# A top-k zone whose weight splits move to GpSimd and whose VectorE queue is written in program order

## The chip, the cores and the metric

The kernel runs on one core of a Trainium2 chip. The metric is the time of one execution on the device, in microseconds (us); the time before is the median of three runs. In the profile PE is TensorE (its weight loads are shown apart, as PEld), DVE is VectorE, ACT is ScalarE, POOL is GpSimd and SP is SyncE, which issues most of the loads.

## The reference

Two layers, each a mixer (a gated linear recurrence and sparse attention) and then an expert retrieval (PEER). Only the second part is cut out here; the change's main work is in its first half. One load of the mixer, the gate weights `lru_wa` and `lru_wx`, is touched too.

```
q = (xf @ wq).reshape(T, 8, 2, 128)                  # T = 256 tokens, 8 heads
s = einsum('thcd,ckd->thck', q, subkeys)             # 128 keys in each half c
sv, si = top_k(s, 16)
cand = sv[:, :, 0, :, None] + sv[:, :, 1, None, :]   # 16 x 16 sums
cv, ci = top_k(cand, 16)
experts = si[0][ci // 16] * 128 + si[1][ci % 16]
gate = softmax(cv)
act = gelu(einsum('cd,ced->ce', xc, u_tab[experts]))
y = einsum('ce,ced->cd', act * gate, v_tab[experts])
```

The layer ends with a residual sum and a layer norm, and the second layer does the same with weights of its own.

## The kernel before

**Dense instead of gathered.** The kernel computes the products with all 16384 rows of `u_tab` (128 tiles of 128 rows, `u_tile(0)` to `u_tile(127)`), keeps their gelu, and later multiplies them with gates that are zero for experts not chosen. So the u tiles depend on no list, and the matmuls of PE can run while DVE makes the lists.

**A weight tile** (`wtile`, L95) is 128x1024 f32. SP loads it into `raw` (four buffers), ACT casts it to `hi` (L104), and another engine subtracts, `lo = raw - hi` (L105); `hi` and `lo` have three buffers each. A narrow tile (`col_mm`, L113) is eight chunks of three matmuls of 256 columns, the third of which reads `lo`; a wide one (`col_mm2`, L122 and L123) is eight chunks of one matmul of 512 columns and one of 256, and DVE adds its two halves (L757). Tiles below `NWIDE` are narrow. The split of a u tile below `NPOOL` and of the weights of queries 2 and 3 is POOL's, every other one DVE's.

**The top-k zone** is what lies inside the pool `topk`. `query(h)` makes the projection of a head, `top(h)` its scores (eight matmuls, L815), a copy of them by ACT into `ss` (L817) and four lists of 16 on DVE, each five operations in `best16` (L801): MAX8, FIND_INDEX8, MATCH_REPLACE8, MAX8, FIND_INDEX8. The profile shows a MATCH_VALUE_LOAD ahead of each of the latter two kinds. For a group of four heads `pairs(g)` adds candidates (nine sums, L829 and L833, into `cd`) and makes eight lists of 50 columns; `choices(g)` does the index work on 2048-element tiles. `turn_round` transposes the results on PE and casts them.

**What sets the order.** `work()` is a generator that issues the zone's work in pieces and yields a cost after each; the loop behind it issues u tiles until these costs are covered:

```
                a, room = 0, 0.0
                for cost in work():
                    room -= cost
                    while room < 0 and a < 96:
                        u_tile(a)
                        room += 2.88 if a < NPOOL else 1.66
```

A scheduler of the language then settles the order on each engine; on DVE operations that do not depend on each other pass one another. Behind the zone comes the dense part, where the gate matrices are built and the other u tiles run.

**The mixer** is issued by a list of tokens per layer, `ORDER[l]`; `d1` calls `const_load(1)`, which loads `lw`, the gate weights of the recurrence (512 KB, L677), and `d2`, `d3` load others. In layer 1 the matmuls at L377 are the first to read `lw`.

Of the kernel before, what the change touches and what calls it, by code (L numbers as in the profile page):

```python
# [16 lines left out]
AF = mybir.ActivationFunctionType  # L17
# [3 lines left out]
D = 1024  # L21
# [28 lines left out]
NPOOL = 14  # L50
NWIDE = 40
# [27 lines left out]
def trunk_kernel(ctx: ExitStack, tc: tile.TileContext, x, xt, cst, lam, pvec, brow, w_in, w_lx, w_v, w_q4, lru_w,  # L79
# [193 lines left out]
    for l in range(NL):  # L273
# [461 lines left out]
        with tc.tile_pool(name="peer", bufs=1, reuse_waits="tile") as pp:  # L735
# [10 lines left out]
            def u_tile(a):  # L746
                if a % 2 == 0:
                    ub[a] = bank() if a < NWIDE else act_tile()
                w = wtile(u_tab[l, a], (8, 128), POOL if a < NPOOL else DVE)
                if a < NWIDE:  # L750
                    ps = ub[a - a % 2]
                    col_mm(ps[:, HALF[a % 2]], w, xT)
                else:
                    ps, at = bank(), ub[a - a % 2]
                    col_mm2(ps, w, xT)
                    ACT.copy(at[:, a % 2], ps[:, S:])  # L756
                    DVE.tensor_tensor(at[:, a % 2], at[:, a % 2], ps[:, :S], op=ALU.add)  # L757
                if a % 2:
                    if a < NWIDE:
                        at = act_tile()  # L760
                        ACT.activation(at.rearrange("p a b -> p (a b)"), ps, AF.Gelu_apprx_tanh)
                    else:
                        ACT.activation(at, at, AF.Gelu_apprx_tanh)  # L763
                    kept[a - 1] = spill.tile([128, 2, S], F32, name="kept%d" % (a - 1), bufs=1)
                    ACT.dma_start(kept[a - 1], at)

            with tc.tile_pool(name="topk", bufs=1, reuse_waits="tile") as tk:
# [17 lines left out]
                def query(h):  # L785
# [4 lines left out]
                    else:  # L790
                        ps = bank()
                        for c in range(2):
                            k = 2 * h + c - 4
                            if "w%d" % k in W:
                                raw_mm(ps[:, c * 256:c * 256 + 256], W["w%d" % k])
                            else:
                                col_mm(ps[:, c * 256:c * 256 + 256], wtile(wq[l, k], (8, 128), POOL if h < 4 else DVE), xT)
# [10 lines left out]
                def top(h):  # L808

                    qh = qhs.pop(h)  # L810
# [6 lines left out]
                    ACT.copy(ss.rearrange("p a b -> p (a b)"), ps)  # L817
                    s2 = tk.tile([128, 4, 128], F32, name="s2", bufs=2)
                    for tb in range(2):
# [75 lines left out]
                def turn_round():  # L895
                    for w in range(3):
# [4 lines left out]
                        tok = ps[:, :256].rearrange("p (q i) -> p q i", i=2)  # L901
# [7 lines left out]
                def work():  # L909
                    for h in (2, 0, 1, 3):  # L910
                        yield from top(h)
                    yield from pairs(0)
                    query(4)
                    yield 2.44 - 5.76
                    for h in range(4, 8):
                        if h < 7:
                            query(h + 1)
                            yield 2.44 - 5.76
                        yield from top(h)
                    yield from pairs(1)  # L920
                    yield from choices(0)
                    yield from choices(1)
                    yield 1.0
# [7 lines left out]
                a, room = 0, 0.0  # L931
                for cost in work():
                    room -= cost
                    while room < 0 and a < 96:
                        u_tile(a)
                        room += 2.88 if a < NPOOL else 1.66
                        a += 1

            with tc.tile_pool(name="dense", bufs=1, reuse_waits="tile") as dp:
# [37 lines left out]

                a0 = a
                made = onehots(0)
                for i in range(32):  # L980
                    following = onehots(8 * i + 8) if i < 31 else None
                    while a < 128 - NLATE and (a - a0) * 32 < (i + 1) * (128 - NLATE - a0):
                        u_tile(a)
# [100 lines left out]
                for a in range(128 - NLATE, 128):  # L1084
                    u_tile(a)
# [211 lines left out]
```

## Time and profile before

| | before |
|---|---|
| runs | 1926.81, 1930.38, 1931.85 us; median 1930.38 |
| profiled execution | 1928.28 us, of which its span is 1926.5 |
| granted TensorE clock, mean over the span | 0.992 |
| busy share of the span | PE 98%, DVE 72%, ACT 53%, POOL 4% |
| longest sums of PE's waits | 20.8 us for `lo` of DVE before L113 (nine waits, longest 4.0), 4.6 for a load before L239, 3.9 before L377 |
| top-k zones | from PE's first narrow u or query tile to its first wide tile: 160.97 to 326.3 us and 1123.03 to 1288.95 us |

A row of a timeline gives start, duration, engine, line, operation, tiles written and read, and in brackets how long the engine was idle before it and who ended that. A group by line gives its count, busy time, mean of one in ns, and the idle time before. A row of a stretch gives the busy time of each engine in it with the count of instructions, then the granted clock as a share of full speed.

### The profile page before, as it was taken

To read this page: it belongs to the slowest core of one execution; us is meant where nothing else is said; L and a number is where in the kernel's file an instruction comes from. 1 tells how busy PE (TensorE), PEld (TensorE's weight loads), DVE (VectorE), ACT (ScalarE), POOL (GpSimd) and SP (SyncE) were. 2 spreads that over 40 slices of the span, in tenths; PEclk is the share of its full clock that TensorE was granted. 3 is DMA by queue.
4 is the path that set the end of the run, shared out by engine and by line. 5 is a ranking of instruction groups with operands and counts; after the bars stand their busy time and mean duration, and the time that the engine had idled before them with its cause. 6 is when DMAs were issued, how large, how long until landed. Compare 5 with 4: busy or idle time off the path is not lost.

```text
span 1926.5 us, 30094 instructions
## 1 busy us (share of the span) xinstructions
PE 1879.1 (98%) x11169; PEld 1595.0 (83%) x11172; DVE 1388.4 (72%) x2729; ACT 1021.4 (53%) x1755; POOL 82.9 (4%) x55
## 2 busy tenths in 40 slices
PE   9999899999999999999999998999999999999998
PEld 8858899888888888888777488998888888888886
DVE  5763994877786766767656639948777767767776
ACT  3635444566666555555445354446666665555553
POOL 0005200000000000000000052000000000000000
PEclk9999999999999999999999999999999999999999
DMA  7505457666668777888362054576666687778783
GB/s 271 173 1 180 159 183 237 200 213 205 208 195 266 240 240 242 287 286 295 132 213 72 0 183 160 183 238 199 212 205 206 198 263 244 240 240 286 252 268 102
DMA packets 130087, 393.76 MB, mean 204 GB/s; under 512 B 15634, under 2 KB 16404, under 8 KB 129812
## 3 DMA queue, kind: packets, MB, share of 16 engines
q1 hardware_dynamic: 111508, 358.28, 58.0%
q10 hardware_dynamic: 18432, 33.56, 4.6%
q8 instruction: 88, 1.44, 0.3%
q14 instruction: 59, 0.48, 0.1%
HBM read 357.18 MB, written 34.60 MB: 203 GB/s over the span
## 4 chain that ended last, share of the span: by engine, by line
PE 87%; DVE 9%; DMA 2%; issue 1%; ACT 1%; POOL 0%; SPq 0%; DVEq 0%; ACTq 0%; POOLq 0%
PE ps L1012 34%; PE ps L122 16%; PE ps L113 13%; PE ps L123 8%; PE ps L971 3%; PE ps L126 3%; PE ps L597 3%; DVE lo L105 2%; DMA raw<-in_v_tab_dram 1%; PE ps L239 1%; PE ps L569 1%; PE ps L522 1%; DVE si L806 1%; DVE cd L829 1%; DVE s L804 1%
## 5 line engine op out<-in xcount | busy, mean ns | idle before, releaser
L105 DVE TENSOR_TENSOR lo<-raw,hi 128x1024 fp32r<-128x1024 f32 x516 | 634.5, 1231 | 291.1 <-ACT hi L104 287.8
L104 ACT CAST hi<-raw 128x1024 fp32r<-128x1024 f32 x548 | 576.3, 1052 | 503.4 <-PE ps L1012 184.9
L1012 PE MATMUL ps<-hi,W 128*128 128x512 f32 x1936 | 518.1, 389 | 0.2 <-ACT hi L104 0.2
L122 PE MATMUL ps<-xT,hi 128*128 128x512 f32 x1408 | 501.2, 400 | 0.0
L1012 PEld LDWEIGHTS ps<-hi,W 128*128 128x128 f32 x1936 | 363.1, 188 | 76.0 <-ACT hi L104 0.6
L123 PE MATMUL ps<-xT,lo 128*128 128x256 f32 x1408 | 392.8, 279 | 1.9 <-DVE lo L105 1.9
L113 PE MATMUL ps<-xT,hi 128*128 128x256 f32 x1984 | 369.2, 288 | 0.0
L113 PEld LDWEIGHTS ps<-xT,hi 128*128 128x128 f32 x1984 | 315.5, 195 | 1.2 <-issue 0.4
L122 PEld LDWEIGHTS ps<-xT,hi 128*128 128x128 f32 x1408 | 264.2, 188 | 60.0
L113 PE MATMUL ps<-xT,lo 128*128 128x256 f32 x992 | 285.2, 288 | 21.4 <-DVE lo L105 20.8
L1012 PE MATMUL ps<-lo,W 128*128 128x512 f32 x968 | 298.0, 389 | 0.5 <-DVE lo L105 0.5
L123 PEld LDWEIGHTS ps<-xT,lo 128*128 128x128 f32 x1408 | 265.3, 188 | 2.8 <-DVE lo L105 2.7
L1012 PEld LDWEIGHTS ps<-lo,W 128*128 128x128 f32 x968 | 181.6, 188 | 38.7 <-DVE lo L105 1.0
L113 PEld LDWEIGHTS ps<-xT,lo 128*128 128x128 f32 x992 | 193.4, 195 | 23.6 <-DVE lo L105 22.6
L1003 ACT CAST W<-act 128x256 fp32r<-128x256 f32 x242 | 96.4, 402 | 96.3 <-PE ps L1012 91.6
L1004 DVE TENSOR_TENSOR W<-act,W 128x256 fp32r<-128x256 f32 x242 | 100.6, 422 | 11.2 <-ACT W L1003 0.9
L757 DVE TENSOR_TENSOR act<-act,ps 128x256 f32<-128x256 f32 x176 | 73.3, 416 | 42.2 <-ACT act L756 41.8
L105 POOL TENSOR_TENSOR lo<-raw,hi 128x1024 fp32r<-128x1024 f32 x32 | 79.6, 2494 | 358.0 <-ACT hi L104 358.0
L763 ACT ACTIVATE act<-act 128x512 f32<-128x512 f32 x88 | 55.7, 633 | 66.2 <-DVE act L757 66.2
L989 DVE TENSOR_TENSOR act<-act,G 128x512 f32<-128x512 f32 x128 | 87.4, 685 | 0.0
L960 DVE TENSOR_TENSOR ohg<-ohg,gT 128x2048 f16<-128x2048 f16 x64 | 78.4, 1225 | 2.0
L975 ACT ACTIVATE G<-ps 128x256 f32<-128x256 f32 x256 | 77.6, 393 | 3.4
(261 smaller groups left out, 1473.8 us busy)
## 6 DMA issues: line engine op xcount, KB each, us to landing
raw<-in_u_tab_dram SPq DMA_DIRECT2D x256, 512.0 KB, 3.7
raw<-in_v_tab_dram SPq DMA_DIRECT2D x256, 512.0 KB, 4.3
kept<-act ACTq DMA_DIRECT2D x128, 256.0 KB, 3.9
act<-kept SPq DMA_DIRECT2D x128, 256.0 KB, 4.2
raw<-in_w_in_dram SPq DMA_DIRECT2D x24, 512.0 KB, 4.2
raw<-in_wq_dram SPq DMA_DIRECT2D x24, 512.0 KB, 3.4
ow<-in_w_out_dram SPq DMA_DIRECT2D x16, 512.0 KB, 8.5
qf<-in_w_q_dram SPq DMA_DIRECT2D x8, 512.0 KB, 3.8
```

The costliest lines, as they stand in the source:

```text
L104: ACT.copy(hi, raw)
L105: lo_eng.tensor_tensor(lo, raw, hi, op=ALU.subtract)
L113: PE.matmul(ps, a[m], b[n], start=start and i == 0, stop=stop and i == 2)
L122: PE.matmul(ps, w[0][:, c], xT[:, c], start=c == 0, stop=False, skip_group_check=True)
L123: PE.matmul(ps[:, :S], w[1][:, c], xT[:, c, 0], start=False, stop=c == NCH - 1, skip_group_check=True)
L757: DVE.tensor_tensor(at[:, a % 2], at[:, a % 2], ps[:, :S], op=ALU.add)
L960: DVE.tensor_tensor(og, oh[:, :, 0:1].to_broadcast([128, 4, 2, 128, 2]), gT[:, qs].unsqueeze(3).to_broadcast([128, 4, 2, 128, 2]), op=ALU. ...
L975: ACT.activation(G[g][:, :, t1:t1 + 4], ps.rearrange("p (t g a) -> p g a t", g=2, a=64)[:, g], AF.Copy, scale=1.0 / GSC)
L989: i = DVE.tensor_tensor(act[a0], act[a0], G[a0 // 64][:, a0 % 64:a0 % 64 + 2, :], op=ALU.mult)
L1003: ACT.copy(whi, at[:, a % 2])
L1004: DVE.tensor_tensor(wlo, at[:, a % 2], whi, op=ALU.subtract)
L1012: PE.matmul(accs[tb * 2 + hf], ww[m][:, TB[tb]], v[n][:, hf * 512:hf * 512 + 512], start=a == first[0] and (m, n) == (0, 0), stop=a == 127 ...
```

## The change

Per layer, in the zone: the split of every u tile and of the weights of queries 3 to 7 goes to POOL until `pairs(1)` is issued, and from there on to DVE (`lo_eng`); before, POOL's were queries 2 and 3 and the u tiles 0 to 13. (Where a query's weights were split early, no split is left.) DVE's instructions stand in program order in the zone (`manual_schedule`). The scores of a head are issued ahead of the lists of the head before it, or in their middle. The transposes of `turn_round` are issued 5.0 us of cost before their casts. All of the zone's u tiles are narrow, and all behind it wide: 46 narrow ones instead of 40. In layer 1 `d1` stands right behind `d0` in the list of tokens.

```diff
-         "c0 I1 I0 d0 d4 P c1 V0 d2 V2 V1 d3 V3 d1 G0 d5 G3 G1 T g1 b0 g0 b1 g2 h0 g3 G2 q2 h1 D S q3 q1 kv q0 "
+         "c0 I1 I0 d0 d1 d4 P c1 V0 d2 V2 V1 d3 V3 G0 d5 G3 G1 T g1 b0 g0 b1 g2 h0 g3 G2 q2 h1 D S q3 q1 kv q0 "
...
-NPOOL = 14
-NWIDE = 40
...
-            def u_tile(a):
-                if a % 2 == 0:
-                    ub[a] = bank() if a < NWIDE else act_tile()
-                w = wtile(u_tab[l, a], (8, 128), POOL if a < NPOOL else DVE)
-                if a < NWIDE:
-                    ps = ub[a - a % 2]
-                    col_mm(ps[:, HALF[a % 2]], w, xT)
-                else:
+            lo_eng = [POOL]
+
+            def u_tile(a, wide=False):
+                w = wtile(u_tab[l, a], (8, 128), lo_eng[0])
+                if wide:
+                    if a % 2 == 0:
+                        ub[a] = act_tile()
                     ps, at = bank(), ub[a - a % 2]
                     col_mm2(ps, w, xT)
                     ACT.copy(at[:, a % 2], ps[:, S:])
                     DVE.tensor_tensor(at[:, a % 2], at[:, a % 2], ps[:, :S], op=ALU.add)
+                else:
+                    if a % 2 == 0:
+                        ub[a] = bank()
+                    ps = ub[a - a % 2]
+                    col_mm(ps[:, HALF[a % 2]], w, xT)
                 if a % 2:
-                    if a < NWIDE:
+                    if wide:
+                        ACT.activation(at, at, AF.Gelu_apprx_tanh)
+                    else:
                         at = act_tile()
                         ACT.activation(at.rearrange("p a b -> p (a b)"), ps, AF.Gelu_apprx_tanh)
-                    else:
-                        ACT.activation(at, at, AF.Gelu_apprx_tanh)
...
-                                col_mm(ps[:, c * 256:c * 256 + 256], wtile(wq[l, k], (8, 128), POOL if h < 4 else DVE), xT)
+                                col_mm(ps[:, c * 256:c * 256 + 256], wtile(wq[l, k], (8, 128), lo_eng[0]), xT)
...
-                def top(h):
-
+                sss = {}
+
+                def scores_of(h):
                     qh = qhs.pop(h)
                     ps = bank()
...
+                    sss[h] = ss
+
+                def top(h, k0=0, k1=4):
+
+                    ss = sss[h]
                     s2 = tk.tile([128, 4, 128], F32, name="s2", bufs=2)
-                    for tb in range(2):
+                    for tb in range(k0 // 2, k1 // 2):
                         for c in range(2):
                             k, j = tb * 2 + c, tb * 4 + h % 4
                             best16(sv[:, h // 4, j, c], si[:, h // 4, j, c], ss[:, k], s2[:, k])
...
+                    turned = []
                     for w in range(3):
                         ps = bank()
                         for tb in range(2):
                             src = ev[:, w, tb] if w < 2 else gate[:, tb]
                             PE.transpose(ps[:, TB[tb]], src.rearrange("p g k -> p (g k)"), ident)
-                        tok = ps[:, :256].rearrange("p (q i) -> p q i", i=2)
+                        turned.append(ps[:, :256].rearrange("p (q i) -> p q i", i=2))
+                    yield 5.0
+                    for w, tok in enumerate(turned):
...
                 def work():
-                    for h in (2, 0, 1, 3):
-                        yield from top(h)
+                    scores_of(2)
+                    scores_of(0)
+                    yield from top(2)
+                    scores_of(1)
+                    yield from top(0)
+                    scores_of(3)
+                    yield from top(1)
+                    query(4)
+                    yield -5.76
+                    yield from top(3)
+                    query(5)
+                    yield -5.76
                     yield from pairs(0)
-                    query(4)
-                    yield 2.44 - 5.76
+                    scores_of(4)
                     for h in range(4, 8):
+                        if h < 6:
+                            query(h + 2)
+                            yield -5.76
+                        yield from top(h, 0, 2)
                         if h < 7:
-                            query(h + 1)
-                            yield 2.44 - 5.76
-                        yield from top(h)
+                            scores_of(h + 1)
+                        yield from top(h, 2, 4)
                     yield from pairs(1)
+                    lo_eng[0] = DVE
                     yield from choices(0)
                     yield from choices(1)
-                    yield 1.0
                     yield from turn_round()
                     yield 4.0
...
-                a, room = 0, 0.0
-                for cost in work():
-                    room -= cost
-                    while room < 0 and a < 96:
-                        u_tile(a)
-                        room += 2.88 if a < NPOOL else 1.66
-                        a += 1
+                a, room = 0, -6.0
+                with tc.manual_schedule(engines={mybir.EngineType.DVE}):
+                    for cost in work():
+                        room -= cost
+                        while room < 0 and a < 96:
+                            u_tile(a)
+                            room += 2.88 if lo_eng[0] is POOL else 1.55
+                            a += 1
...
+                if a % 2:
+                    u_tile(a)
+                    a += 1
...
-                        u_tile(a)
+                        u_tile(a, True)
...
-                u_tile(a)
+                u_tile(a, True)
```

DVE, a head's lists in layer 0; `ss` are the scores, `sv` and `si` the values and indices found, `s_1469` the scratch copy. Before:

```order
L802 MAX sv<-ss 128x8 x2
L803 MAX_INDEX si<-sv,ss 128x8
L804 MATCH_REPLACE s_1593<-sv,ss 128x128
L803 MAX_INDEX si<-sv,ss 128x8
L805 MAX sv<-s_1593 128x8
L804 MATCH_REPLACE s_1593<-sv,ss 128x128
L806 MAX_INDEX si<-sv,s_1593 128x8
L805 MAX sv<-s_1593 128x8
```

The same place in the changed kernel, where these lines are 804 to 808:

```order
L804 MAX sv<-ss 128x8
L805 MAX_INDEX si<-sv,ss 128x8
L806 MATCH_REPLACE s_1667<-sv,ss 128x128
L807 MAX sv<-s_1667 128x8
L808 MAX_INDEX si<-sv,s_1667 128x8
```

Where operations of two lists alternated, one list's five now follow each other.

DVE, the end of the second group's lists in layer 0; `cv`, `ci` and `c_1364` belong to the lists of `pairs(1)`, the rows from `gt` to `ge` to `choices(0)`, and `lo` is a split. Before:

```order
L804 MATCH_REPLACE c_1364<-cv,cd 128x50
L105 TENSOR_TENSOR lo<-raw,hi 128x1024
L805 MAX cv<-c_1364 128x8
L862 COPY dsi<-sif 128x8
L863 TENSOR_TENSOR dsi<-sif 128x8x15
L806 MAX_INDEX ci<-cv,c_1364 128x8
L851 TENSOR_TENSOR gt<-cv 128x128
L861 CAST cif<-ci 128x128
L868 TENSOR_TENSOR ge<-cif,i_130 128x2048
L105 TENSOR_TENSOR lo<-raw,hi 128x1024
```

The same place in the changed kernel, where L103 is the split:

```order
L807 MAX cv<-c_1364 128x8
L808 MAX_INDEX ci<-cv,c_1364 128x8
L859 TENSOR_TENSOR gt<-cv 128x128
L868 CAST sif<-si 128x256
L869 CAST cif<-ci 128x128
L870 COPY dsi<-sif 128x8
L871 TENSOR_TENSOR dsi<-sif 128x8x15
L872 COPY dst<-i_130 128x1
L873 TENSOR_TENSOR dst<-i_130 128x15
L103 TENSOR_TENSOR lo<-raw,hi 128x1024
L876 TENSOR_TENSOR ge<-cif,i_130 128x2048
```

The `lo` here is that of u tile 18, the first split of DVE in the zone; before, splits stood among the lists.

SP, the loads of layer 1's mixer. Before:

```order
L675 DMA cmix<-in_cst_dram 128x936
L681 DMA cw_9549<-in_cmp_w_dram 64x192
L679 DMA cw1a<-in_cmp_w_dram 128x1024
L679 DMA cw1b<-in_cmp_w_dram 128x1024
L677 DMA lw<-in_lru_w_dram 128x1024
```

The same place in the changed kernel:

```order
L673 DMA cmix<-in_cst_dram 128x936
L675 DMA lw<-in_lru_w_dram 128x1024
L679 DMA cw_9589<-in_cmp_w_dram 64x192
L677 DMA cw1a<-in_cmp_w_dram 128x1024
L677 DMA cw1b<-in_cmp_w_dram 128x1024
```

The load of `lw` moved ahead of three others, two of which have its size.

## Rows read from the trace of the kernel before

**Rows 1.** Page, busy time, share and instructions of each engine.

```profile
PE 1879.1 (98%) x11169; PEld 1595.0 (83%) x11172; DVE 1388.4 (72%) x2729; ACT 1021.4 (53%) x1755; POOL 82.9 (4%) x55
```

**Rows 2.** Groups by line, PE, 160.9 to 325 and 1123.5 to 1287 us.

```profile
L113 PE MATMUL ps<-xT,lo 128*128 128x256 f32 x396 | 114.0, 288 | 10.0 <-DVE lo L105 10.0
...
L113 PE MATMUL ps<-xT,lo 128*128 128x256 f32 x394 | 113.5, 288 | 10.7 <-DVE lo L105 10.1 <-POOL lo L105 0.6
```

**Rows 3.** Stretches: us, busy of PE PEld DVE ACT POOL, PEclk, DMA, GB/s.

```profile
160.90:325.00 164.10, 154.07 (x1257) 153.07 (x1256) 130.19 (x492) 77.55 (x95) 37.43 (x15) 0.98 0.61 199
230.00:240.00 10.00, 7.83 (x53) 7.63 (x52) 10.00 (x42) 2.09 (x2) 3.51 (x1) 0.83 0.35 109
```

**Rows 4.** Timeline of PE: start, us, line, operation, shapes, idle before.

```profile
220.94 0.98 PEld L815 LDWEIGHTS ps<-skt,qh 128*128 128x128 f32 x8
...
318.03 0.40 PE L113 MATMUL ps<-xT,hi 128*128 128x256 f32 x2
...
318.39 0.40 PE L113 MATMUL ps<-xT,hi 128*128 128x256 f32 x2
...
403.02 0.40 PE L122 MATMUL ps<-xT,hi 128*128 128x512 f32 x1
...
403.37 0.40 PE L122 MATMUL ps<-xT,hi 128*128 128x512 f32 x1
```

**Rows 5.** Timeline of POOL, layer 0.

```profile
177.81 2.40 POOL L105 TENSOR_TENSOR lo<-raw,hi 128x1024 fp32r<-128x1024 f32 x1 [0.49 <-ACT hi L104]
...
232.72 3.51 POOL L105 TENSOR_TENSOR lo<-raw,hi 128x1024 fp32r<-128x1024 f32 x1 [7.57 <-ACT hi L104]
```

**Rows 6.** Timeline of DVE, lists, layer 0.

```profile
178.76 0.49 DVE L802 MAX8 sv<-ss 128x8 f32<-128x128 f32 x2 [4.10 <-ACT ss L817]
...
182.54 0.29 DVE L806 FIND_INDEX8 si<-sv,s 128x8 uint32<-128x128 f32 x1
182.74 0.08 DVE L804 MATCH_VALUE_LOAD s<-sv,ss 128x8 f32 x1
182.80 0.28 DVE L804 MATCH_REPLACE8 s<-sv,ss 128x128 f32<-128x128 f32 x1
183.11 0.30 DVE L805 MAX8 sv<-s 128x8 f32<-128x128 f32 x1
183.44 0.09 DVE L806 MATCH_VALUE_LOAD si<-sv,s 128x8 f32 x1
...
201.51 0.20 DVE L804 MATCH_REPLACE8 c<-cv,cd 128x50 f32<-128x50 f32 x1
```

**Rows 7.** Timeline of DVE, sums and splits, layer 0.

```profile
197.88 2.88 DVE L829 TENSOR_TENSOR cd<-sv 128x128 f32<-128x128 f32 x6
...
234.12 3.19 DVE L105 TENSOR_TENSOR lo<-raw,hi 128x1024 fp32r<-128x1024 f32 x1
...
256.92 0.72 DVE L829 TENSOR_TENSOR cd<-sv 128x128 f32<-128x128 f32 x6
257.56 1.22 DVE L105 TENSOR_TENSOR lo<-raw,hi 128x1024 fp32r<-128x1024 f32 x1
```

**Rows 8.** Timeline of ACT, layer 0.

```profile
184.30 0.59 ACT L817 COPY ss<-ps 128x512 f32<-128x512 f32 x1
```

**Rows 9.** Timeline of SP, its DMA issues, layer 1.

```profile
981.22 0.58 SPq L679 DMA_DIRECT2D cw1a<-in_cmp_w_dram  x1
...
982.63 0.33 SPq L677 DMA_DIRECT2D lw<-in_lru_w_dram  x1
```

**Rows 10.** DMA issues, 980.9 to 983 us: KB each, median us to landing.

```profile
cw1a<-in_cmp_w_dram SPq DMA_DIRECT2D x1, 512.0 KB, 7.0
...
lw<-in_lru_w_dram SPq DMA_DIRECT2D x1, 512.0 KB, 8.2
```

**Rows 11.** Timeline of PE, start of layer 1.

```profile
990.92 5.26 PE L377 MATMUL ps<-xc,lw 128*128 128x256 f32 x12 [3.89 <-DVE lo L105]
```

**Rows 12.** Stretches, as Rows 3.

```profile
990.00:1000.00 10.00, 9.07 (x42) 7.99 (x43) 2.48 (x4) 3.53 (x8) 0.00 (x0) 0.71 0.92 304
```

## The prediction

> **What bounds the kernel now.** I read the busy row first: PE is busy 98% of the span, DVE 72%, POOL 4% [rows 1]. So only what leaves PE waiting, or slows it, can be won. The list of PE's waits, split by stretch, comes second. In the top-k zone of layer 0 (160.9 to 325 us) PE sat idle 10.0 us before matmuls that read a `lo` half of DVE, in that of layer 1 10.7 us, 0.6 of it for POOL [rows 2]; the reader should see that one line, the split, is behind nearly all of it. Third, the granted clock: over the zone of layer 0 it is 0.98 of full speed, which over 164.1 us is 3.3 us of work lost, and the stretch 230 to 240 us shows where: 0.83, so 1.7 us lost in one drop from 2.4 to 1.2 GHz, after a wait [rows 3]. For layer 1 I take the same 3.3 us. What can be won in the zones is thus 10.0 + 3.3 = 13.3 us and 10.7 + 3.3 = 14.0 us.
>
> Why does DVE come late with a split? It does two jobs that do not need each other: the lists (MAX8, FIND_INDEX8, MATCH_REPLACE8) and the splits that feed PE. From tile 14 on, the splits stand in its queue among lists and 2048-element index work.
>
> **What PE asks for.** A chunk of a narrow tile starts 0.36 us after the one before (318.03, 318.39), so a narrow tile takes 8 x 0.36 = 2.88 us; a chunk of a wide tile 0.35 us, so 2.80; the scores of a head 0.98 us [rows 4]. Before, 40 u tiles a layer are narrow, after, 46 (the zone's), so PE pays 6 x 0.08 = 0.5 us a layer, 1 us in all.
>
> **POOL's part.** It now splits 28 tiles a layer, not 16: q3's two, q4's to q7's eight and u tiles 0 to 17. A split takes 2.40 us and POOL idled 0.49 us before it for ACT's cast, which is just PE's 2.88 us rhythm [rows 5]: POOL keeps pace with 0.48 us a tile in hand. The longest split took 3.51 us; it ran against a DVE split that took 3.19 us [rows 5, 7]. In the list phase no DVE split is left, so I charge PE nothing here. The cover is three `hi`/`lo` buffers; if every split took 3.51 us, PE would lose 0.63 us on each of 26 tiles, 16.4 us a layer.
>
> **DVE's lists in program order.** This is what the change adds. Now, the operations of four lists alternate: a head's four lists begin at 178.76 us and end at 183.8 (the last load, 183.44 + 0.09, and a FIND_INDEX8 of 0.28 us), 1.26 us each. The last one shows what an operation costs that needs the one just before it: MATCH_REPLACE8 to MAX8 0.31 us (182.80, 183.11), MAX8 to the load of its match values 0.33 us (183.44), that load 0.09; an independent next one follows FIND_INDEX8 after 0.20 us, and MATCH_REPLACE8 its load after 0.06 [rows 6]. In program order a list is MAX8, FIND_INDEX8, MATCH_REPLACE8, MAX8, FIND_INDEX8: 0.33 + 0.09 + 0.20 + 0.06 + 0.31 + 0.33 + 0.09 + 0.20 = 1.6 us, a head 6.4 us. With 50 columns an operation is 0.08 us shorter (0.20 against 0.28 us [rows 6]), five of them 0.4: 1.2 us, the eight of a group 9.6 us.
>
> The sums of `pairs` are two-input DVE work. Six of them took 2.88 us with POOL at work and 0.72 us without [rows 7]. Nine alone are 1.1 us; they wait for at least one POOL split, 2.40 us, and two at most, as POOL leaves gaps of only 0.49 us: 3.5 to 5.9 us, or 1.1 us if they fall into a longer gap. I take 3.5, the nearest to the six. `pairs(1)` now pays this too.
>
> The rule of the Trainium skill that would speak against my 1.6 us stands in VectorE: DVE Perf Modes, section The DRAIN you can't avoid: the next operation waits for the pipe to empty in any case, and a semaphore wait after each costs nothing extra. By it a list in program order would cost what the alternating one costs, and PE would not wait at all (second rival). The rows here are against it: 0.20 us without a dependence, 0.31 and 0.33 with one.
>
> **Where the two meet.** PE goes on with tiles 0 to 17 and the queries without DVE; from tile 18 on DVE splits again, and that split stands behind the whole list work. Count from the end of head 6's scores. PE has tile 10, head 7's scores, tiles 11 to 17, and the two matmuls of tile 18 that read only `hi`: 8 x 2.88 + 0.98 + 0.24 = 24.3 us. DVE: ACT's copy of the scores, 0.59 us [rows 8], with handover 0.7; heads 6 and 7, 12.8; sums 3.5; eight lists 9.6; seven small index operations, about 1 us as an estimate from MATCH_REPLACE8 at 0.2 us for 50 columns; the split, 1.22 us [rows 7]. Together 28.8 us. PE waits 4.5 us. Earlier lists hardly move this: a head's 6.4 us fits into PE's 2 x 2.88 + 0.98 = 6.7 us between two scores, so head 6 starts when PE lets it. Queued behind the split are the index work and the next splits; ACT's exponential of the gates also waits for the list's end, with the casts of tiles 19 and 20 behind it. Tile 19's split comes after a 2048-element compare, 2.4 us as an estimate from the split's 1.22 for 1024 elements; with the split 3.6 us against a tile's 2.88, so 0 to 0.7 us more, I take 0.5. After that compares, splits and shorter work alternate, and I charge nothing more.
>
> The wait probably costs one drop of the clock, 1.7 us as above. Per layer 4.5 + 0.5 + 1.7 = 6.7 us stay (7.3 with layer 1's 0.6 for POOL): won are 13.3 - 6.7 = 6.6 and 14.0 - 7.3 = 6.7 us. Bounds of the wait: lists as cheap as now (1.26 and 0.86 us) and sums at 1.1 us take 2.7 + 2.7 + 2.4 us off, so no wait; sums at 5.9 us make it 6.9 us.
>
> **The weights of the gates in layer 1.** `d1`, the load of `lw`, moves from behind `cw`, `cw1a` and `cw1b` on SP's queue to the front of them. It was issued at 982.63 us [rows 9] and landed 8.2 us later [rows 10], at 990.8; PE restarts with the matmuls that read it at 990.92 after 3.89 us idle [rows 11]. So the wait named there for DVE is one for this DMA. `cw1a`, which stood two places ahead, landed at 981.22 + 7.0 = 988.2 us; `lw` in front of it lands then or earlier, and PE was ready at 987.03: 0 to 1.2 us stay, I take 0.6, so 3.3 us won. From 990 to 1000 us the clock was 0.71 [rows 12], 2.9 us lost; with a shorter wait between none and all of it comes back; I take 2. Together 5.3 us. `cw1a` and `cw1b` land later by one transfer; their readers come after three more projection tiles, 8.6 us of PE work, which hide it.
>
> The other edits cost nothing: scores issued a head early, loads in another order, transposes 5 us ahead of their copies. They hide behind PE's queue of ready tiles; if one came late, PE would lose at most a tile's 2.88 us each time.
>
> **Sum.** 6.6 + 6.7 + 5.3 - 1.0 = 17.6 us off the profiled execution's 1928.3 us: 1910.7. That execution lies 2.1 us under the median of the three runs, 1930.4, so 1911 to 1913; I say 1911. Against 1930.4, 0.3% (5.8 us) is about what a measurement of this kernel tells from no change.
>
> **Rivals.** One: the wait stays under 7 us, as above, 1903 to 1917; chance 0.57. Two: lists in program order cost what they cost now, PE never waits for tile 18: 6.7 us more won per layer, 1897; for it, that the rows show one list's end alone [rows 6], where the 0.31 and 0.33 us may have another reason; against it those two rows; chance 0.17. This is where the rule of the Trainium skill in VectorE: DVE Perf Modes ends. Three: the wait is 7 to 12 us, or the clock drops twice, or `lw` wins nothing: 1917 to 1924; 0.13. Four, no change: POOL becomes PE's pace at 3.51 us; the 16.4 us a layer eat the zone's 13.3 and 14.0, and `lw` is left: about 1930; for it the one 3.51 us row, against it every split beside lists at 2.40; 0.06. Five, slower: each of the nine sums of `pairs(0)` waits for a whole POOL split, 9 x 2.4 = 21.6 us in place of 3.5. The heads behind it slip by 18 us, POOL has then finished, so `pairs(1)` pays 1.1: PE waits 4.5 + 18.1 - 2.4 = 20.2 us and the layer loses 22.4 instead of 13.7, so 1928.3 + 2 x 8.7 - 4.3 = 1941; it decides from about six waits in nine on. For it: 0.72 us became 2.88 beside POOL; against it: over six sums that is about one split's time, not six [rows 7]; chance 0.07. The Trainium skill, SBUF — State Buffer, section Who interferes with whom, speaks for it: whoever issues first holds the shared port for its whole instruction.
>
> The range to 8 in 10 is 1894 to 1922: cases one, two and most of three. Faster by over 0.3% are one to three, 0.87; within 0.3% four, 0.06; slower five, 0.07.
>
> **What would show it.** Right: POOL 28 splits a layer at about 2.4 us beside the lists; each list 1.6 us; no PE wait in a zone but one of 3 to 6 us at tile 18, with a `lo` of DVE as its end; the wait before the gate matmuls of layer 1 under 1.3 us. Wrong: PE waits named for POOL, sums of `pairs` at several splits' time, waits in the second half of the zone, where DVE runs index work between splits in a fixed order with about 4 us to spare.

## The result and the profile after

Four runs of the changed kernel took 1909.68 to 1911.65 us, median 1911.21; the kernel before beside them 1931.12. The ratio is 0.990, with a 95% interval of 0.9883 to 0.9917. The profiled execution took 1909.68 us, its span is 1907.9, 18.6 us under that of before. In this document a time of an experiment is the median of its runs, and each is given with its ratio to the kernel before, which ran beside it on the same chip. The medians of the kernel before lie between 1928.5 and 1931.1 us, and single executions of one kernel lie further apart, so a difference of less than about 3 us between two medians says little; where it matters, I compare the lengths of stretches in the traces.

Engine busy time, answering [rows 1]:

```profile
PE 1873.5 (98%) x11268; PEld 1596.0 (84%) x11268; DVE 1390.6 (73%) x2693; ACT 1017.9 (53%) x1743; POOL 138.6 (7%) x79
```

POOL has 56 us more. Next, as in [rows 2], the groups of PE that read a `lo` of DVE in the two zones (163.2 to 340.9 and 1110.8 to 1289 us):

```profile
L111 PE MATMUL ps<-xT,lo 128*128 128x256 f32 x448 | 127.8, 285 | 6.5 <-DVE lo L103 6.5
...
L111 PE MATMUL ps<-xT,lo 128*128 128x256 f32 x448 | 128.0, 286 | 6.5 <-DVE lo L103 6.5
```

Each zone now has 6.5 us of idle time before this line, where it had 10.0 and 10.7. The timeline of PE shows that it is one wait in each zone; its first, middle and last rows here are the wait of layer 0, a restart among the gate matmuls of layer 1, which answers to [rows 11], and the wait of layer 1:

```profile
258.18 0.58 PE L111 MATMUL ps<-xT,lo 128*128 128x256 f32 x1 [6.48 <-DVE lo L103]
...
983.55 1.99 PE L375 MATMUL ps<-xc,lw 128*128 128x256 f32 x8 [0.71 <-DVE xc L369]
...
1205.82 0.58 PE L111 MATMUL ps<-xT,lo 128*128 128x256 f32 x1 [6.48 <-DVE lo L103]
```

What DVE does before that wait, at the end of the lists in layer 0 (start, duration, engine, line, operation):

```profile
236.54 0.27 DVE L804 MAX8 sv<-ss 128x8 f32<-128x128 f32 x1
...
238.11 0.28 DVE L804 MAX8 sv<-ss 128x8 f32<-128x128 f32 x1
...
241.25 5.30 DVE L837 TENSOR_TENSOR cd<-sv 128x128 f32<-128x128 f32 x8
246.47 0.21 DVE L841 TENSOR_TENSOR cd<-sv 128x64 f32<-128x64 f32 x1
246.71 0.21 DVE L804 MAX8 cv<-cd 128x8 f32<-128x50 f32 x1
...
247.90 0.19 DVE L804 MAX8 cv<-cd 128x8 f32<-128x50 f32 x1
...
256.03 0.27 DVE L859 TENSOR_TENSOR gt<-cv 128x128 f32<-128x128 f32 x1
...
256.91 1.22 DVE L103 TENSOR_TENSOR lo<-raw,hi 128x1024 fp32r<-128x1024 f32 x1
```

A list starts 1.57 us after the one before (236.54, 238.11), one of 50 columns 1.19 us (246.71, 247.90), those behind it 1.16. The nine sums between them take 5.46 us, from 241.25 to the first MAX8 at 246.71; eight of them are merged into the row of 5.30 us. The view by tile gives their shortest, median and longest in ns:

```profile
L837 DVE TENSOR_TENSOR cd<-sv x8: 168/186/2426, 241.2 to 244.1; 128x16 f32<-128x16 f32 x3, 128x128 f32<-128x128 f32 x1, 128x64 f32<-128x64 f32 x1, 128x40 f32<-128x40 f32 x1
```

Two of the eight are long, the first with 2.34 us and the last with 2.43; the six between them take 0.17 to 0.21 us each. POOL's timeline shows what ran beside them, two splits, and each of the two long sums ends with one of them:

```profile
241.03 2.41 POOL L103 TENSOR_TENSOR lo<-raw,hi 128x1024 fp32r<-128x1024 f32 x1 [0.47 <-ACT hi L102]
243.91 2.60 POOL L103 TENSOR_TENSOR lo<-raw,hi 128x1024 fp32r<-128x1024 f32 x1 [0.47 <-ACT hi L102]
```

The split of tile 18 starts only at 256.91, right behind the lists and the small index work. ACT's timeline shows a second engine that stood still:

```profile
247.23 1.28 ACT L860 ACT_TABLE_LOAD   x1
256.34 0.31 ACT L860 ACTIVATE gt<-gt 128x128 f32<-128x128 f32 x1 [7.83 <-DVE gt L859]
...
256.79 1.99 ACT L102 CAST hi<-raw 128x1024 fp32r<-128x1024 f32 x2
```

After loading its table, ACT waits 7.83 us for DVE's subtraction `gt` and only then casts the two next tiles.

The clock, by the view of stretches as in [rows 3, 12]:

```profile
163.28:340.90 177.62, 171.14 (x1418) 170.79 (x1417) 147.04 (x496) 85.50 (x104) 65.15 (x27) 0.98 0.63 207
258.00:262.00 4.00, 3.82 (x19) 3.82 (x20) 4.00 (x4) 2.67 (x3) 0.00 (x0) 0.54 0.40 134
990.00:1000.00 10.00, 10.00 (x96) 9.72 (x96) 8.73 (x20) 5.35 (x13) 0.00 (x0) 1.00 0.82 283
```

From 258 to 262 us it is 0.54: after the wait PE runs at 1.2 GHz for some 3.5 us. In the gate matmuls of layer 1 it is 1.00, where it was 0.71. The load of `lw` is issued at 975.64 us and takes 5.3 us; it lands at 980.9, ahead of the first gate matmul (981.8), and the 0.71 us for which PE still waits among them end with DVE's `xc`, the other input of these matmuls: a wait of its own that the load's wait had covered:

```profile
975.64 0.43 SPq L675 DMA_DIRECT2D lw<-in_lru_w_dram  x1
```

```profile
lw<-in_lru_w_dram SPq DMA_DIRECT2D x1, 512.0 KB, 5.3
cw1a<-in_cmp_w_dram SPq DMA_DIRECT2D x1, 512.0 KB, 6.9
```

**Where the 18.6 us come from.** I take the first and last starts of groups of PE in both traces. From the first narrow tile of a zone to the first matmul of the gates' part (L1012 before, L1039 after), layer 0 went from 445.2 to 438.7 us and layer 1 from 445.8 to 439.3: 6.5 us won in each. From the first projection matmul of layer 1 to its zone it went from 143.4 to 136.3: 7.1. Layer 0's last part gave 0.9 (373.5 to 372.6), as in e12, where nothing of it is changed. The start of layer 0 took 2.3 us more, though nothing there was changed: between 60 and 80 us the clock is 0.91 where the execution of before shows 1.00.

```profile
60.00:80.00 20.00, 18.46 (x138) 17.88 (x137) 14.18 (x23) 12.81 (x19) 0.00 (x0) 0.91 0.48 155
```

Of the 14 profiled executions of this document 12 show 0.91 in this stretch, among them that of e12, which differs from the kernel before only in layer 1. It is the execution of before that was spared the drop, and with it e11's.

### The profile page after: what moved, and what is told of

Read it like the earlier page. It is cut to its first block, busy times and chain, and to the rows that moved or that the text cites. A ratio compares the mean times of both kernels' runs of the same rounds, so it can differ in the third digit from the quotient of the medians.

```text
span 1907.9 us, 30269 instructions
## 1 busy us (share of the span) xinstructions
PE 1873.5 (98%) x11268; PEld 1596.0 (84%) x11268; DVE 1390.6 (73%) x2693; ACT 1017.9 (53%) x1743; POOL 138.6 (7%) x79
## 4 chain that ended last, share of the span: by engine, by line
PE 93%; DVE 4%; DMA 1%; ACT 1%; issue 0%; SPq 0%; DVEq 0%; ACTq 0%
PE ps L1039 35%; PE ps L111 18%; PE ps L120 16%; PE ps L121 8%; PE ps L995 3%; PE ps L595 3%; PE ps L124 3%; PE ps L237 1%; PE ps L567 1%; DMA raw<-in_v_tab_dram 1%; PE ps L520 1%; PE ps L144 1%; PE ps L818 1%; DVE cd L837 1%; PE ps L547 0%
## 5 line engine op out<-in xcount | busy, mean ns | idle before, releaser
L103 DVE TENSOR_TENSOR lo<-raw,hi 128x1024 fp32r<-128x1024 f32 x492 | 601.5, 1224 | 263.4 <-ACT hi L102 259.5
L1039 PE MATMUL ps<-hi,W 128*128 128x512 f32 x1936 | 517.8, 389 | 0.0
L120 PE MATMUL ps<-xT,hi 128*128 128x512 f32 x1312 | 467.3, 400 | 0.0
L1039 PEld LDWEIGHTS ps<-hi,W 128*128 128x128 f32 x1936 | 363.2, 188 | 75.6
L111 PE MATMUL ps<-xT,hi 128*128 128x256 f32 x2176 | 401.6, 287 | 0.0
L111 PEld LDWEIGHTS ps<-xT,hi 128*128 128x128 f32 x2176 | 343.5, 194 | 1.2 <-issue 0.4
L1039 PE MATMUL ps<-lo,W 128*128 128x512 f32 x968 | 298.0, 389 | 0.1
L120 PEld LDWEIGHTS ps<-xT,hi 128*128 128x128 f32 x1312 | 246.3, 188 | 56.0
L1039 PEld LDWEIGHTS ps<-lo,W 128*128 128x128 f32 x968 | 181.6, 188 | 38.1 <-DVE lo L103 0.5
L103 POOL TENSOR_TENSOR lo<-raw,hi 128x1024 fp32r<-128x1024 f32 x56 | 135.1, 2414 | 313.6 <-ACT hi L102 313.6
L754 DVE TENSOR_TENSOR act<-act,ps 128x256 f32<-128x256 f32 x164 | 68.4, 417 | 48.6 <-ACT act L753 48.2
```

The lines of the kernel that those rows point to most:

```text
L103: lo_eng.tensor_tensor(lo, raw, hi, op=ALU.subtract)
L111: PE.matmul(ps, a[m], b[n], start=start and i == 0, stop=stop and i == 2)
L120: PE.matmul(ps, w[0][:, c], xT[:, c], start=c == 0, stop=False, skip_group_check=True)
L1039: PE.matmul(accs[tb * 2 + hf], ww[m][:, TB[tb]], v[n][:, hf * 512:hf * 512 + 512], start=a == first[0] and (m, n) == (0, 0), stop=a == 127 ...
```

## The experiments

Each kernel is the changed kernel with the edit shown, if nothing else is said. The line numbers of rows are those of each kernel.

**e1_d1_back: the load at its old place.**

```diff
-         "c0 I1 I0 d0 d1 d4 P c1 V0 d2 V2 V1 d3 V3 G0 d5
+         "c0 I1 I0 d0 d4 P c1 V0 d2 V2 V1 d3 V3 d1 G0 d5
```

> The changed kernel with the load of lw in layer 1 issued where it stood before, behind cw, cw1a and cw1b. Theory (the load landed 3.9 us late and the wait cost a drop of the clock as well): PE waits 3 to 4 us before the gate matmuls of layer 1, and the time is 5 to 7 us above the changed kernel, 1916 to 1918 us. Rival (the mixer of layer 1 became faster for another reason, and the load was hidden anyway): within 2 us of the changed kernel, no such wait.

1916.45 us, ratio 0.9934 (0.9918 to 0.9951). PE's timeline names the load itself this time:

```profile
984.95 5.46 PE L375 MATMUL ps<-xc,lw 128*128 128x256 f32 x12 [3.71 <-DMA lw<-in_lru_w_dram]
```

The theory holds: the wait is 3.71 us, and 5.2 us of time are lost by the medians.

**e12_d1_alone: only this load moved, in the kernel before.** The edit is the reverse of e1's, applied to the kernel before.

> The kernel before with the earlier load of lw in layer 1 as its only change. Theory (the parts add up; taken out of the changed kernel this part cost about 5 us): 5 to 7 us under the kernel before of the same chip, a ratio of about 0.997, PE's wait before the gate matmuls of layer 1 under 1 us. Rival (the wait is given back later in the mixer, since cw1a and cw1b land later): within 2 us of the kernel before.

1923.71 us against 1928.53, ratio 0.9976 (0.9966 to 0.9985): 4.8 us, just under the 5 to 7 expected.

```profile
988.90 2.00 PE L377 MATMUL ps<-xc,lw 128*128 128x256 f32 x8 [0.50 <-DVE xc L371]
```

The wait of 3.89 us [rows 11] is 0.50. So this part adds up by itself, about 5 us either way. What PE waits for now is again `xc`.

**e8_pool_16: program order with POOL's old share.**

```diff
-                w = wtile(u_tab[l, a], (8, 128), lo_eng[0])
+                w = wtile(u_tab[l, a], (8, 128), POOL if a < 14 else DVE)
...
-                                col_mm(ps[:, c * 256:c * 256 + 256], wtile(wq[l, k], (8, 128), lo_eng[0]), xT)
+                                col_mm(ps[:, c * 256:c * 256 + 256], wtile(wq[l, k], (8, 128), POOL if h < 4 else DVE), xT)
```

> The changed kernel with the 16 splits of POOL that it had before (u tiles 0 to 13, query 3, the rest DVE's, in program order among the lists). Theory (POOL's extra splits are what frees PE from the lists): waits for DVE's splits come back at several places of the list phase, 10 to 20 us a layer, 1920 to 1945 us. Rival (program order, which keeps the first group's index work behind the lists, gave the gain, and POOL's extra splits little): 1908 to 1916.

1927.47 us, ratio 0.9993 (0.9984 to 1.0003). The waits for DVE are back at several places of the zone, the two longest in layer 0 being

```profile
220.35 0.58 PE L111 MATMUL ps<-xT,lo 128*128 128x256 f32 x1 [4.70 <-DVE lo L103]
...
252.08 0.58 PE L111 MATMUL ps<-xT,lo 128*128 128x256 f32 x1 [2.08 <-DVE lo L103]
```

It is the theory's mechanism, but smaller: 16 us for both layers, where it said 10 to 20 for each. By the measure of the section above its zones take 446.9 and 448.0 us, against 438.7 and 439.3 in the changed kernel and 445.2 and 445.8 before. So they are slower than those of before, and the load's 5 us make up for that.

**e4_scheduler: POOL's new share without program order.**

```diff
-                with tc.manual_schedule(engines={mybir.EngineType.DVE}):
+                if True:
```

> The changed kernel with DVE's order in the zone left to the scheduler, which alternates lists and puts the split of tile 18 behind one 2048-element compare and two multiplications. Theory (DVE's wait is the sum of what stands ahead of that split): lists about 5 us shorter, 4.7 us of index work ahead of the split, so a wait of 6 to 7 us as in program order, 1909 to 1913 us; program order then gave nothing by itself and POOL's splits gave the zone's gain. Rival (program order is what gave the gain): waits of PE at several places in the zone as before the change, 1918 to 1925 us.

1950.67 us, ratio 1.0106 (1.009 to 1.0123), slower than before; its zones take 458.0 and 457.2 us. My theory fell, and the rival's 1918 to 1925 was too low as well. The scheduler had put the first group's index work between the lists, beside POOL's splits. DVE's timeline shows six additions of that work in one row:

```profile
219.07 11.48 DVE L851 TENSOR_TENSOR t<-t 128x1024 f16<-128x1024 f16 x6
```

**e10_index_early: is it that work?** Program order is kept, and `choices(0)` is issued whole behind the first group's lists.

```diff
                     yield from pairs(0)
+                    for _ in choices(0):
+                        pass
                     scores_of(4)
...
-                    yield from choices(0)
+                    for n in (1.2, 2.3, 2.2, 1.5, 2.3, 1.6, 2.3, 1.2, 1.8):
+                        yield n
                     yield from choices(1)
```

> The changed kernel, in program order, but with the whole index work of the first group (choices 0) put right behind the first group's lists, where the scheduler had put it too; tiles and their splits stay where they are. Theory (two-input index work beside POOL's splits is what made the scheduler's order slow): its operations take about twice their time, ACT's casts wait behind its exponential there, and PE waits in the middle of the zone; 1930 to 1955 us. Rival (that order was slow because of the other operations it moved, or of the alternating lists): 1909 to 1916.

1959.61 us, ratio 1.0152 (1.0137 to 1.0168), above the theory's range; the zones take 463.2 and 464.2 us. DVE's timeline has three additions of `choices` beside POOL's splits and, later, three of the same shapes without them (POOL was idle for 15 us then):

```profile
220.30 7.83 DVE L851 TENSOR_TENSOR t<-t 128x1024 f16<-128x1024 f16 x3
...
242.08 1.60 DVE L851 TENSOR_TENSOR t<-t 128x1024 f16<-128x1024 f16 x3
```

7.83 us against 1.60. PE's longest waits in layer 0:

```profile
252.10 0.80 PE L111 MATMUL ps<-xT,hi 128*128 128x256 f32 x2 [8.13 <-ACT hi L102]
...
281.63 0.58 PE L111 MATMUL ps<-xT,lo 128*128 128x256 f32 x1 [7.51 <-DVE lo L103]
```

The first of these waits stands at the end of a chain that ACT's timeline shows:

```profile
250.52 0.59 ACT L820 COPY ss<-ps 128x512 f32<-128x512 f32 x1 [15.46 <-DVE s L806]
251.00 1.05 ACT L102 CAST hi<-raw 128x1024 fp32r<-128x1024 f32 x1
```

A copy of scores waits 15.46 us for DVE's lists, which stand behind the index work, and the cast for PE stands behind the copy. So the place of the index work is enough to make an order as slow as the scheduler's. How its parts share the loss was not tested: the work occupies DVE for 31 us here (213.82 to 244.87), of which about 14.7 are lost beside POOL, as an estimate from rows of the same timeline with POOL idle (3.25, 7.83, 2.50 and 5.94 us against 1.23, 1.60, 0.39 and 1.60). The rest would stand ahead of the second group's lists in any case, and the exponential, which moved along, holds up casts of its own.

**e9_sums_twice: what the sums lose to POOL.** The first group's nine sums are issued twice.

```diff
-                    DVE.tensor_tensor(cd[:, :, OFF[8]:NCAND], a[:, :, 8:16],
-                                      b[:, :, 0:1].to_broadcast([128, 8, 8]), op=ALU.add)
+                    for n in range(2 - g):
+                        DVE.tensor_tensor(cd[:, :, OFF[8]:NCAND], a[:, :, 8:16],
+                                          b[:, :, 0:1].to_broadcast([128, 8, 8]), op=ALU.add)
+                    for i in range(8 - 8 * g):
+                        DVE.tensor_tensor(cd[:, :, OFF[i]:OFF[i] + CNT[i]], a[:, :, i:i + 1].to_broadcast([128, 8, CNT[i]]),
+                                          b[:, :, :CNT[i]], op=ALU.add)
```

> The changed kernel with the nine sums of the first group issued twice (the second time they write the same values), where POOL splits without a break. Theory (a sum that meets a split waits until that split ends, and only what fits into POOL's gaps runs, so 18 sums meet twice as many splits): the 18 sums take about 10.5 us in place of 5.4, DVE carries about 5 us to the handover, PE's wait at tile 18 grows from 6.5 to about 11 us, 1919 to 1923 us. Rival (the sums lose two splits whatever their number): they take 6.5 us, PE waits 7 to 8 us, 1911 to 1914.

1914.1 us (1909.72 to 1917.73), ratio 0.992 (0.99 to 0.9939). DVE's timeline:

```profile
200.33 5.39 DVE L837 TENSOR_TENSOR cd<-sv 128x128 f32<-128x128 f32 x8
205.64 0.47 DVE L842 TENSOR_TENSOR cd<-sv 128x64 f32<-128x64 f32 x2
206.03 5.42 DVE L845 TENSOR_TENSOR cd<-sv 128x128 f32<-128x128 f32 x8
...
245.94 1.41 DVE L837 TENSOR_TENSOR cd<-sv 128x128 f32<-128x128 f32 x8
```

On the sums the theory holds: eight take 5.39 us, eight more 5.42. On the time it failed; the 1914.1 us lie beside the rival's 1911 to 1914, though the rival had the sums wrong. The heads behind slipped so far that the second group's sums came when POOL was nearly done, and took 1.41 us in place of 5.30. PE's wait grew by 0.6 us only:

```profile
258.99 0.58 PE L111 MATMUL ps<-xT,lo 128*128 128x256 f32 x1 [7.11 <-DVE lo L103]
```

**e2_alternate: two lists side by side.** `best16x2` issues each of the five operations for two lists before the next.

```diff
+                def best16x2(p, q):
+                    for v, ix, src, tmp in (p, q):
+                        DVE.max(v[:, 0:8], src)
+                    for v, ix, src, tmp in (p, q):
+                        DVE.max_index(ix[:, 0:8], v[:, 0:8], src)
...
-                        best16(cv[:, g, j], ci[:, g, j], cd[:, j], c2[:, j])
+                        best16x2(*[(cv[:, g, k], ci[:, g, k], cd[:, k], c2[:, k]) for k in (j, j + 1)])
```

> The changed kernel with two lists written side by side, operation by operation, still in program order. Theory (an operation that needs the one just before it costs 0.1 us more, and these gaps make DVE late at u tile 18): a list falls from 1.57 us to about 1.25, one of 50 columns from 1.16 to about 0.85, so two heads and eight short lists end about 5 us earlier; PE's wait at tile 18 falls from 6.5 us to 1 or 2 in each layer, and with the drop of the clock 10 to 14 us are won, 1897 to 1901 us. Rival (the wait is set by POOL's splits, which hold up the sums, or by the casts): the wait stays over 5 us and the time at 1909 to 1912.

1908.44 us, ratio 0.9891 (0.9875 to 0.9908). Nearly nothing won, where the theory had 10 to 14 us, and yet DVE was in time. PE now waits for a cast of ACT and the split behind it:

```profile
250.58 0.50 PE L111 MATMUL ps<-xT,hi 128*128 128x256 f32 x2 [3.00 <-ACT hi L102]
...
253.01 0.58 PE L111 MATMUL ps<-xT,lo 128*128 128x256 f32 x1 [1.93 <-POOL lo L103]
```

**e3_three_more: POOL splits tiles 18 to 20 too.**

```diff
                     yield from pairs(1)
+                    yield 3 * 2.88
                     lo_eng[0] = DVE
```

> The changed kernel with three more u tiles split by POOL before DVE takes over (tiles 18 to 20, 8.64 us of PE's work). Theory (DVE is late by 6.5 us because the handover comes at tile 18 while the lists last longer than planned): no wait of PE in the zones, the drop of the clock there gone too, 14 to 16 us won, 1895 to 1898 us. Rival one (POOL, which now splits while the first index operations run, holds these up by up to 2.4 us each): a wait of 1 to 4 us at tile 21, 1899 to 1905. Rival two (the wait only moves to tile 21 whole): 1909 to 1912.

1910.73 us, ratio 0.9904 (0.9887 to 0.992). The time is rival two's, but not its mechanism: what PE waits for is again ACT, then POOL.

```profile
256.97 0.71 PE L111 MATMUL ps<-xT,hi 128*128 128x256 f32 x2 [3.55 <-ACT hi L102]
...
259.40 0.58 PE L111 MATMUL ps<-xT,lo 128*128 128x256 f32 x1 [1.72 <-POOL lo L103]
```

```profile
246.31 1.28 ACT L860 ACT_TABLE_LOAD   x1
255.42 0.31 ACT L860 ACTIVATE gt<-gt 128x128 f32<-128x128 f32 x1 [7.83 <-DVE gt L859]
...
255.88 1.99 ACT L102 CAST hi<-raw 128x1024 fp32r<-128x1024 f32 x2
```

In ACT's timeline the exponential of the gates had been put ahead of these casts; it waits 7.83 us for DVE's `gt`, and then two casts follow.

**e5_exp_late: the exponential later.** The two lines that make `gt` move to the middle of the index work.

```diff
-                    DVE.tensor_tensor(gt, cv[:, g], cv[:, g, :, 0:1].to_broadcast([128, 8, 16]), op=ALU.subtract)
-                    ACT.activation(gt, gt, AF.Exp)
...
                     tree(of(ev[:, 0], g), t1)
                     yield 1.5
+                    DVE.tensor_tensor(gt, cv[:, g], cv[:, g, :, 0:1].to_broadcast([128, 8, 16]), op=ALU.subtract)
+                    ACT.activation(gt, gt, AF.Exp)
```

> The changed kernel with the subtraction of gt and its exponential moved from the head of the index work to the middle of it, so that ACT's casts of tiles 19 and later no longer stand behind the end of the lists; the handover stays at tile 18. Theory (two engines are late at once: DVE with the split of tile 18, and ACT, whose exponential waits for the lists with casts behind it; either alone holds PE): the wait of 6.5 us for DVE's split stays, 1908 to 1912 us. Rival (ACT's blocked queue alone is the cause): the wait goes, 1895 to 1900.

1910.63 us, ratio 0.991 (0.9893 to 0.9926), with a wait of 6.2 us for DVE's split in each layer, as the theory said. In layer 0:

```profile
257.53 0.58 PE L111 MATMUL ps<-xT,lo 128*128 128x256 f32 x1 [6.25 <-DVE lo L103]
```

**e6_three_more_exp_late and e7_alternate_exp_late: e5's edit with e3's, and with e2's.**

> Both edits together: POOL splits tiles 18 to 20 too, and the exponential of the gates stands later. Theory (both engines were late): no wait over 1 us in the zones, the drop of the clock gone, 14 to 17 us won against the changed kernel, 1894 to 1898 us. Rival (POOL's splits now run beside index operations with two inputs and hold them up): a wait of 2 to 5 us at tile 21, 1900 to 1907.

> Two lists side by side, with the exponential moved as above; the handover stays at tile 18. Theory (the lists' end 5 to 7 us earlier reaches PE only when ACT's queue is free too): PE's wait at tile 18 0 to 2 us, 1897 to 1903 us. Rival (alternating gains nothing that PE sees): 1908 to 1912.

e6: 1896.51 us, ratio 0.9829 (0.9812 to 0.9845). The stretch from 160 to 350 us has PE busy throughout, at full clock:

```profile
160.00:350.00 190.00, 190.00 (x1563) 188.71 (x1562) 150.72 (x500) 94.10 (x115) 74.47 (x31) 1.00 0.65 218
```

e7: 1897.66 us, ratio 0.9844 (0.9827 to 0.986). PE stands still for 0.4 us in all in the same stretch:

```profile
160.00:350.00 190.00, 189.58 (x1549) 186.49 (x1548) 143.73 (x510) 97.20 (x126) 65.26 (x27) 1.00 0.63 215
```

Four lists of a head begin in two pairs, 2.36 us apart, so a list costs 1.18 us:

```profile
226.94 0.49 DVE L812 MAX8 sv<-ss 128x8 f32<-128x128 f32 x2 [1.87 <-ACT ss L832]
...
229.30 0.47 DVE L812 MAX8 sv<-ss 128x8 f32<-128x128 f32 x2
```

Both as the theory expected. The medians have 0.5 to 2.8 us won by each edit alone, which is not clear of their noise, and 14 to 15 by each pair. The two zones together, in the traces, take 878.0 us in the changed kernel; 875.9 in e2, 877.0 in e3 and 877.0 in e5; 861.3 in e6 and 862.7 in e7. So one edit alone wins 1 to 2 us there, and a pair 15 to 17.

**e11_alternate_two_more_exp_late.** All three, with two more tiles for POOL (`2 * 2.88`).

> The changed kernel with lists side by side, two more tiles split by POOL, and the exponential later. If PE's waits in the zones are the whole of what can still be won there, this gives what either of the two earlier ways gave, 1894 to 1898 us; if the lists' end still costs something that no wait shows, 1890 or less.

1894.67 us (1890.32 to 1894.92), ratio 0.9815 (0.9801 to 0.9828): the best version, 16.5 us under the changed kernel by the medians, 17.0 in the two zones.

```profile
160.00:350.00 190.00, 190.00 (x1560) 187.93 (x1559) 142.51 (x506) 96.72 (x122) 70.91 (x30) 1.00 0.63 216
```

PE stands still nowhere in this zone; what the lists still cost is hidden.

## Why the prediction was right

**The load of `lw`** was forecast at 5.3 us: 3.3 of wait and 2 of clock. The two experiments measure 5.2 and 4.8 by the medians. In the traces the mixer of layer 1 takes 5.7 us more with the load back at its old place (e1, 142.0 against 136.3) and 5.4 less with nothing but the load moved (e12, 138.0 against 143.4). The pair of before and after shows 7.1, because the execution of before has one more drop of the clock there, which that of after has not:

```profile
1020.00:1030.00 10.00, 9.18 (x61) 8.80 (x61) 9.36 (x15) 6.27 (x9) 0.00 (x0) 0.83 0.32 105
```

Such a drop comes and goes between executions: of the 12 with the earlier load six take 136.3 us, five 137.8 to 138.0 and one 139.5. My 0.6 us of wait that stays came out at 0.71, but by chance: I had the load land up to 1.2 us too late, it landed 0.9 us ahead of PE, and what stays is the wait for `xc`, which I did not see.

**The lists** were forecast at 1.6 and 1.2 us and took 1.57 and 1.16 to 1.19. Set side by side they take 1.18 (e7), so what an operation pays for needing the one before it is real: about 0.4 us a list. The rule of the Trainium skill that I weighed (VectorE: DVE Perf Modes, section The DRAIN you can't avoid) would have made both the same, as I read it; here the measurement decides against that for these operations. The section itself adds that a next operation that is not held starts earlier, which my reading left out.

**The wait at tile 18** was forecast at 4.5 us and is 6.48. Head 6's copy ends at 228.6 and its lists start at 228.67, after 0.26 us in which DVE stood still, so PE does set where it begins, as the prediction said, though only just. The term that was mis-sized is the sums of `pairs(1)`: I took 3.5 us, one split of POOL, from a range of 3.5 to 5.9; they took 5.46, two splits. That is 2.0 us, the whole difference. All else came within 0.7 and nearly cancels: the handover took 1.4 us for 0.7 (PE is done with the scores at 227.3; ACT copies a query first), the lists are 0.5 us cheaper together. The two long sums show why it is near the upper bound, and e9 that it is so each time they are issued: they lose two splits. Each long sum ends with the split that was under way when it came. This agrees with the Trainium skill, SBUF — State Buffer, section Who interferes with whom (whoever issues first holds the shared port for its whole instruction), as far as one operation goes; that every sum would lose a split of its own, the fifth rival, is excluded by 5.46 us.

**Second split and clock.** I had 0.5 us for tile 19 and 1.7 for one drop of the clock. There is no second wait, and the drop costs about 1.5 us: five and a half chunks at 0.64 in place of 0.36 us, by PE's timeline after 258.18. So 8.0 us stay per layer where I had 6.7. The zones nevertheless won 6.5 each, where 6.1 and 6.2 follow from the forecast: in the waits of before there is a further 0.9 us per layer for a wide tile's `lo` (L123) that my 10.0 and 10.7 us did not count, and it went too. With it 5.7 and 5.8 follow; in layer 1 the 0.6 us of wait for POOL, which the forecast let stand, is gone as well, and 0.8 us of layer 0 stay open.

**POOL** kept pace: 28 splits a layer at 2.4 to 2.6 us, no wait of PE for it. The fourth rival needed 3.51.

**What the prediction did not see** is what the parts do to each other. It took program order for a cost alone. Taken away (e4), the kernel is 39 us slower; POOL's extra splits taken away (e8), 16 us. Each without the other loses in the zones: against before, 24.3 us in e4 and 4.0 in e8, both layers together. Program order is worth so much because it keeps the two-input index work behind the point where POOL stops; e10 shows what it costs ahead of it. What the smaller parts are worth, the earlier scores and transposes and the narrow tiles, was not tested. And the forecast named the split of tile 18 as the one thing that PE waits for, with the exponential and the casts only "queued behind"; e2, e3 and e5 to e7 show two engines late at the same place, so that freeing one wins 1 to 2 us in the zones and freeing both 15 to 17.

That the total came out at 1911 thus owes something to luck, to errors that cancel: 1.3 us a layer too little left against 0.9 not counted as won, and, between the two profiled executions, 2.3 us for a drop of the clock that before was spared against 1.4 for one that after was spared and 0.9 won in layer 0's last part.

## What to carry to other kernels

Before two engines share work, ask of each operation that may run beside the other's whether both can slow down: here one edit pays only because another keeps such operations apart, so neither can be judged alone. When a wait is named for one engine, look what the other engines in the chain do in the same microseconds; if one of them stands still too, the first fix will mostly move the wait and hardly shorten it. A blocking instruction that needs a far-off result (here an exponential) belongs behind the short work that others wait for; here this paid only together with a second edit against the late split of DVE.

## What the runs showed of the hardware

Beside back-to-back splits of POOL three two-input additions of DVE took 7.83 us, without them 1.60 (e10). The lists did not feel POOL: a short list started every 1.16 us in the changed kernel both beside splits (212.72 to 213.88 us) and after the last one (247.90 to 249.06). POOL itself lost little beside single sums: its longest split in the changed kernel took 2.60 us, the median 2.41. Beside the index work of e10, four splits took 3.1 us each:

```profile
215.45 12.39 POOL L103 TENSOR_TENSOR lo<-raw,hi 128x1024 fp32r<-128x1024 f32 x4 [8.45 <-ACT hi L102]
```
